# Copying each row of a column roll in three pieces instead of two

## Chip, cores, metric

One core of one Trainium2 chip. The metric is device time in microseconds, the median over runs. A ratio is the mean time of one kernel's fast runs over the mean of the fast runs of the kernel before from the same rounds on the same chip; it is therefore not quite the ratio of the medians quoted beside it. The bracket after a ratio is its 95% interval. A difference counts as faster or slower from 2% on.

## The reference

```python
x = np.random.randn(8192, 8192).astype(np.float32)   # 268 MB
shift = 100
np.roll(x, shift, axis=1)
```

Each row of 32768 B moves 400 B to the right, and its last 400 B come round to the front.

## The kernel before

There is no arithmetic and no on-chip buffer, only copies from HBM to HBM. Rows are taken in 16 chunks of 512, whose copies are issued by turns from two engines (SP and ACT, one DMA queue each). Every chunk has a long piece and a short piece.

```python
    s = shift % n_cols                      # 100
    engines = [nc.sync, nc.scalar]
    n_chunks = 16
    rows_per_chunk = n_rows // n_chunks     # 512
    for i in range(n_chunks):
        r0 = i * rows_per_chunk
        r1 = r0 + rows_per_chunk
        eng = engines[i % 2]
        eng.dma_start(out=out[r0:r1, s:], in_=x[r0:r1, : n_cols - s])
        eng.dma_start(out=out[r0:r1, :s], in_=x[r0:r1, n_cols - s:])
# ... launch code left out ...
```

In bytes, per row: a long piece of 32368 B is written from byte 400 of the output row to its end, and a short piece of 400 B is written to bytes 0 to 400. Byte 400 is 12.5 x 32. In what follows an edge of a write is called *even* if it falls on a multiple of 32 B of the output, and *ragged* if it does not. All ragged edges here are 16 B off. (Edges are counted from the start of a row. Rows are 32768 B long, and the tensor itself is taken to start on a multiple of 32 B; its address is not recorded.)

## Time and profile before

| | before |
|---|---|
| time before the prediction, median of 3 | 850.75 us (848.87 to 853.41) |
| span of the profiled run | 830.1 us |
| copied | 268.44 MB at 323 GB/s (647 GB/s read plus written) |
| long packets, 8192 of 32368 B | mean 1568 ns, 12% of them at 1199 ns |
| short packets, 8192 of 400 B | mean 35 ns, most at 24 ns |

The packet lines are worked out from the trace's packet records, which give each packet's queue, size, start and duration. Here one packet is one piece of one row. The profiled run is 20 us shorter than the timed runs; its chip is not recorded.

From the page of the kernel before: the span, the slices (busy tenths of the DMA engines and GB/s in 40 equal slices), the packets, the two queues (packets, MB, share of 16 engines' span) and the HBM traffic.

```profile
span 830.1 us, 77 instructions
...
DMA  9999999999999999999999999999999999999996
GB/s 306 324 326 315 328 322 323 331 329 328 334 323 334 338 311 340 324 334 334 306 339 324 332 329 314 328 331 335 329 305 335 332 328 326 311 334 328 329 326 208
DMA packets 16896, 268.44 MB, mean 323 GB/s; under 512 B 8704, under 2 KB 8704, under 8 KB 8704
...
q1 hardware_dynamic: 8448, 134.22, 49.8%
q10 hardware_dynamic: 8448, 134.22, 49.1%
HBM read 268.44 MB, written 268.44 MB: 647 GB/s over the span
```

The engines are hardly ever idle: 49.8% and 49.1% of their span add to 98.9%. A long packet takes 1199 ns at its quickest and 1568 ns in the mean. The GB/s row has shallow dips about every fifth slice, where chunks end (311, 306, 314, 305, 311; the first two chunk ends do not show at this width).

The chain of waits shows nothing here (0% in every entry): the only computing engine with any work is POOL, with 0.2 us. The timeline shows why issuing is not the limit. Its columns are start, duration, engine and line:

```profile
2.02 0.62 SPq L33 DMA_DIRECT2D out_dram<-in_x_dram  x1
2.28 0.85 ACTq L33 DMA_DIRECT2D out_dram<-in_x_dram  x1
2.69 94.08 SPq L34 DMA_DIRECT2D out_dram<-in_x_dram  x1
```

The third line is the fourth issue on SP. It lasts 94 us. What it waits for is not shown, but the DMA engines are working all that time: from 2.69 to 96.77 us the windows view gives a DMA share of 1.00 and 325 GB/s.

The first dip in stretches of 8 us, from the windows view of the kernel before (stretch, its length, POOL busy, clock, mean DMA share of the 16 engines, GB/s):

```profile
core 0: us, POOL busy (x), PEclk, DMA share, GB/s
88.00:96.00 8.00, 0.00 (x0) 1.00 0.93 332
96.00:104.00 8.00, 0.00 (x0) 1.00 0.99 308
104.00:112.00 8.00, 0.00 (x0) 1.00 1.06 294
112.00:120.00 8.00, 0.00 (x0) 1.00 0.98 344
120.00:128.00 8.00, 0.00 (x0) 1.00 1.06 348
...
102.00:110.00 8.00, 0.00 (x0) 1.00 1.01 237
```

The dip at 96 to 112 us is where the first two chunks end and their 1024 short packets run. Afterwards the rate is above the mean of 323 GB/s for a while (344 and 348), so little is lost. The view counts a packet, its bytes and its whole duration, in the stretch in which it starts; that is one way in which a share can pass 1 (the records also overlap). So where a stretch is cut matters: the last line, asked for separately, lies 2 us off the grid and shows 237 GB/s at the same dip.

### The profile page before, as it was taken

Reading aid. Unit: us, or ns where it says so; the run is one execution under the profiler, and the core shown is the slowest. Engines: PE = TensorE matmul, PEld = TensorE weight load, DVE = VectorE, ACT = ScalarE, POOL = GpSimd, SP = SyncE. Lnnn points to the kernel's source line nnn. Section 1 sums busy time; section 2 is a strip of 40 time slices with the busy share of each in tenths; the row PEclk is TensorE's granted clock in tenths of the full one; section 3 lists DMA queues with packets and bytes.
Section 4 is the critical chain, followed back from the end, with each engine's and each line's share of the span. In section 5 each row is a group of like instructions: output and inputs, shape, how many; then the busy total and the mean of one; then the engine's idle time right before and its main releaser. Section 6 shows DMA issues by size and latency. Waiting matters only on the chain. (4 is left out here: it accounts for less than half of the span.)

```text
span 830.1 us, 77 instructions
## 1 busy us (share of the span) xinstructions
POOL 0.2 (0%) x4
## 2 busy tenths in 40 slices
POOL 0000000000000000000000000000000000000000
DMA  9999999999999999999999999999999999999996
GB/s 306 324 326 315 328 322 323 331 329 328 334 323 334 338 311 340 324 334 334 306 339 324 332 329 314 328 331 335 329 305 335 332 328 326 311 334 328 329 326 208
DMA packets 16896, 268.44 MB, mean 323 GB/s; under 512 B 8704, under 2 KB 8704, under 8 KB 8704
## 3 DMA queue, kind: packets, MB, share of 16 engines
q1 hardware_dynamic: 8448, 134.22, 49.8%
q10 hardware_dynamic: 8448, 134.22, 49.1%
HBM read 268.44 MB, written 268.44 MB: 647 GB/s over the span
## 5 line engine op out<-in xcount | busy, mean ns | idle before, releaser
L51 POOL MEMSET const-bfloat16-1.0<- 128x1 bf16 x1 | 0.1, 102 | 0.0
L51 POOL MEMSET const-uint8-127<- 128x1 uint8 x1 | 0.1, 102 | 0.0
L51 POOL MEMSET const-float32-0.0<- 128x1 f32 x1 | 0.1, 99 | 0.2 <-issue 0.2
L51 POOL MEMSET const-float32-1.0<- 128x1 f32 x1 | 0.1, 99 | 0.0
## 6 DMA issues: line engine op xcount, KB each, us to landing
out_dram<-in_x_dram SPq DMA_DIRECT2D x8, 16184.0 KB, 206.1
out_dram<-in_x_dram ACTq DMA_DIRECT2D x8, 16184.0 KB, 206.3
out_dram<-in_x_dram ACTq DMA_DIRECT2D x8, 200.0 KB, 205.8
out_dram<-in_x_dram SPq DMA_DIRECT2D x8, 200.0 KB, 205.6
```

The costliest lines, as they stand in the source:

```text
L51: nc = _bacc.Bacc("TRN2", target_bir_lowering=False, num_devices=1)
```

## The change

The intent is a long piece that begins on a 512 B boundary of the output row. The 28 columns (112 B) from byte 400 to byte 512 become a third piece. The long piece is then 32256 B, and its source starts 112 B into the input row.

```diff
     s = shift % n_cols
+    a = -(-s // 128) * 128
+    pieces = [(a, a - s, n_cols - a), (0, n_cols - s, s), (s, 0, a - s)]
     engines = [nc.sync, nc.scalar]
     n_chunks = 16
-    rows_per_chunk = n_rows // n_chunks
+    rows = n_rows // n_chunks
     for i in range(n_chunks):
-        r0 = i * rows_per_chunk
-        r1 = r0 + rows_per_chunk
-        eng = engines[i % 2]
-        eng.dma_start(out=out[r0:r1, s:], in_=x[r0:r1, : n_cols - s])
-        eng.dma_start(out=out[r0:r1, :s], in_=x[r0:r1, n_cols - s:])
+        r = slice(i * rows, (i + 1) * rows)
+        for d, c, n in pieces:
+            if n > 0:
+                engines[i % 2].dma_start(out=out[r, d:d + n], in_=x[r, c:c + n])
```

(Blank lines and one comment that also changed are left out.)

## The prediction

> **What bounds the kernel now.** Data movement alone: the page's busy table shows 0.2 us of compute, and the queue lines put 49.8% and 49.1% of the 16 engines' span on the two queues, so the engines are never without work. The page gives 323 GB/s copied, 647 GB/s read plus written. The trace's packet records (one per row piece) say what the work is:
>
> - 8192 packets of 32368 B: 1199 ns at the shortest (12% of them), 1568 ns in the mean. Summed over 16 engines, 803 us.
> - 8192 packets of 400 B: 24 ns in most, 35 ns in the mean: 18 us.
>
> At their shortest these packets would need 626 us, an estimate from those durations[...].
>
> **What the change does.** The long piece of each row becomes 32256 B and starts on a 512 B boundary of the output; its source now starts 112 B into the row. The 400 B piece stays. A third piece of 112 B per row is added: 8192 more packets, 16 more DMA issues.
>
> - Hoped for: no ragged start of the long write. [...]32368 B at 1199 ns and 400 B at 24 ns differ by 27.2 B/ns[...]. The ragged boundary at byte 400 is still written from both sides. I expect almost no gain.
> - Long packets shorter by 112 B: 4 ns x 8192 / 16 = -2 us.
> - Added 112 B packets: estimate 13 ns at the shortest, from the 27.2 B/ns, and 25 ns with the stalls that the 400 B packets show: 8192 x 13..25 ns / 16 = +7 to +13 us. [...]around 100 us, in the short pieces, the rate falls from about 325 to 230 to 250 GB/s for 8 us.
>
> **On the critical path:** the engines are 98.9% busy, so the net +5 to +11 us lands on it, except where long packets[...] speed up in turn. Issue does not count: each sequencer waits 77 to 96 us per chunk.
>
> **Prediction:** 856 us (before: 850.75), 80% range 822 to 880. Faster by over 2%: 0.15; within 2%: 0.62; slower by over 2%: 0.23.
>
> **What would show the steps.** Right: packet records with 8192 of 112 B at 13 to 30 ns; long packets still near 1560 ns mean, shortest 1194 ns; longer GB/s dips at chunk boundaries. Wrong: the mean long packet well under 1540 ns, or GB/s outside the dips above 335: alignment matters all along the row.
>
> **What would make it wrong.** [...]small writes may cost far more than their engine time, or fewer chunks in flight (three pieces share the same number of completion semaphores) may leave engines idle at chunk boundaries: 2 to 4% slower.

The sum: -2 us for the shorter long packets and +7 to +13 us for the added ones make +5 to +11 us, and 856 us is the lower end, 850.75 + 5.

## More of the kernel before

The runs fell on several chips. The kernel before took 833 us on chip 15, 840 us on chips 9 and 0, and 852 us in the rounds of the result, whose chip is not recorded. Only ratios are compared across chips.

## The result and the profile after

| | before | after |
|---|---|---|
| median of 4 | 851.7 us (848.87 to 853.41) | 875.93 us (872.49 to 879.06) |
| ratio | | 1.0289 [1.0246, 1.0331], slower |

The same lines of the page, for the changed kernel:

```profile
span 876.7 us, 93 instructions
...
DMA  9999999999999999999999999999999999999995
GB/s 303 328 315 324 283 299 318 333 324 259 303 325 322 322 258 313 325 328 330 250 323 324 321 325 249 336 318 325 327 238 344 316 325 324 238 338 311 328 319 156
DMA packets 25344, 268.44 MB, mean 306 GB/s; under 512 B 17152, under 2 KB 17152, under 8 KB 17152
...
q1 hardware_dynamic: 12672, 134.22, 50.9%
q10 hardware_dynamic: 12672, 134.22, 48.5%
HBM read 268.44 MB, written 268.44 MB: 612 GB/s over the span
```

Between the dips the rate is about what it was, 299 to 344 GB/s in the slices. The dips are still every fifth slice, but now at 283, 259, 258, 250, 249, 238 and 238. The first of them in the windows view of the changed kernel:

```profile
core 0: us, POOL busy (x), PEclk, DMA share, GB/s
88.00:96.00 8.00, 0.00 (x0) 1.00 0.94 302
96.00:104.00 8.00, 0.00 (x0) 1.00 1.01 326
104.00:112.00 8.00, 0.00 (x0) 1.00 1.20 143
112.00:120.00 8.00, 0.00 (x0) 1.00 0.95 302
120.00:128.00 8.00, 0.00 (x0) 1.00 1.00 339
```

For 8 us the core moves 143 GB/s (237 in the lowest such stretch shown before), with a DMA share of 1.20. The engines are not idle; their packets take longer: in the packet records of the whole run 133 long packets took more than 3 us, against 2 before.

To compare runs, the time lost at the chunk boundaries is worked out from the packet records. It is the length of each stretch that holds short packets (with 8 us on either side) less the bytes moved in it over 325 GB/s. The sum is over the first seven boundaries; the eighth is the end of the run.

| | before | after |
|---|---|---|
| lost at seven boundaries | 4 us | 39 us |
| long packets: mean, total over 16 engines | 1568 ns, 803 us | 1625 ns, 832 us |
| 400 B packets: mean, total over 16 | 35 ns, 18 us | 44 ns, 23 us |
| 112 B packets: mean, total over 16 | none | 31 ns, 16 us |

So most of the added time went to the boundaries: 35 of the 46.6 us between the two profiled spans. Of the packet time that was added, 29 us lie in long packets and 16 us in the new packets themselves. The first profile flatters the kernel before, though. Profiled again (below), it lost 10 us at the seven boundaries and the changed kernel 34, and the rate outside the boundaries was 329 to 330 GB/s in both.

### The profile page after: what moved, and what is told of

Same layout as the page of the kernel before. It is cut to its first block, busy times and chain, and to the rows that moved or that the text cites. A ratio compares the mean times of both kernels' runs of the same rounds, so it can differ in the third digit from the quotient of the medians.

```text
span 876.7 us, 93 instructions
## 1 busy us (share of the span) xinstructions
POOL 0.2 (0%) x4
## 2 busy tenths in 40 slices
DMA packets 25344, 268.44 MB, mean 306 GB/s; under 512 B 17152, under 2 KB 17152, under 8 KB 17152
## 3 DMA queue, kind: packets, MB, share of 16 engines
HBM read 268.44 MB, written 268.44 MB: 612 GB/s over the span
```

## The experiments

The rival theories were these. (1) The added packets cost, and alignment of the long piece is worth nothing. (2) The moved misalignment costs, since the long read now starts ragged. (3) Alignment gains, but less than the packets cost. (4) With three issues per chunk and the same completion semaphores, fewer chunks are in flight. (Both traces show eight such semaphores, and four issues on each engine before the first long wait: on SP the fourth ends at 96.8 us before and at 97.6 us after.) If (1) held, the question was which property of the packets costs: number, size, edges or bunching. All edits below are to the list of pieces, (first output column, first input column, columns), in a loop like that of the changed kernel, unless said otherwise. The diffs are shortened and written against the changed kernel. The first four expectations name absolute times for a kernel before of 851 us; on the faster chip their results are read as ratios.

### The kernel before, profiled again: before_again

No edit.

> The kernel before, unchanged, for a second profile: the first profile's span (830 us) is about 20 us under the spans of its timed runs, so it may flatter the comparison. All theories: the time again near 851 us. The loss of moved bytes at each chunk boundary should again be under 2 us of time in the trace, against about 5 us in the changed kernel; if it is 4 us or more here, the boundaries are not what tells the two apart.

Measured: 836.38 us in one run, state unknown, on a chip where the kernel before had a median of 833.19 us. The boundaries lost 10 us in all, 0.9 to 2.2 us each. That is more than in the first profile (4 us) and far less than in the changed kernel (39 us), so the boundaries do tell the two apart. The time was not near 851 us as expected, on this other chip. The first profile's short span therefore says little; its chip is not known.

### The 112 B cut off at the other end: cut_at_end

```diff
-    pieces = [(128, 28, 8064), (0, 8092, 100), (100, 0, 28)]
+    pieces = [(100, 0, 8064), (0, 8092, 100), (8164, 8064, 28)]
```

> Same three sizes per row (32256, 400, 112 B) in the same order, but the 112 B are cut off at the row's end, so that the long piece still starts ragged at byte 400 of the output row and aligned in the input. Theory 1 (the added packets cost, alignment is worth nothing): as slow as the changed kernel, 870 to 880 us. Theory 2 (the moved misalignment costs: the long read now starts ragged): as fast as before, 848 to 858 us. Theory 3 (alignment gains, and the added packets cost even more): slower than the changed kernel, over 885 us.

Measured: 850.34 us against 833.19, ratio 1.020 [1.0152, 1.0247]. The absolute 870 to 880 us was written for a slower chip; as a ratio the result is close to the changed kernel's (1.0225 when that was run again, below). Here the long read is aligned again, and the kernel is still slow, so theory (2) falls. The boundaries lost 27 us. On this one chip the span grew by 14.3 us over before_again and the loss at the boundaries by 16 us, so the boundaries hold all of the difference.

### Without the third piece: no_third

```diff
-    pieces = [(128, 28, 8064), (0, 8092, 100), (100, 0, 28)]
+    pieces = [(128, 28, 8064), (0, 8092, 100)]
```

> The changed kernel without its 112 B piece; 28 columns of the output stay unwritten, so the result is wrong on purpose. Theory 1: as the kernel before within 1%, 843 to 857 us, and dips at the chunk boundaries as shallow as before's. Theory 2: still slower than before, 865 us or more. Theory 3: faster than before by over 2%, under 833 us.

The result is wrong (28 columns unwritten). Measured: 825.75 us against 833.19, ratio 0.9933 [0.9877, 0.999]. It moves 0.34% fewer bytes (28 of 8192 columns), which alone would give 0.9966 if time went with bytes (an estimate). The rest, 0.3%, is inside the interval. The long piece aligned to 512 B, with its read made ragged, thus gains nothing net that this run resolves, and by the interval's lower end at most about 0.9%. (Taken as an absolute time, 825.75 us would have met theory 3's "under 833 us"; but on this chip the kernel before itself takes 833 us.) Theory (3) falls, and the cost lies in the third piece. The boundaries lost 8 us, as in the kernel before.

### A third piece of 512 B with even edges: third_512

```diff
-    pieces = [(128, 28, 8064), (0, 8092, 100), (100, 0, 28)]
+    pieces = [(100, 0, 7964), (0, 8092, 100), (8064, 7964, 128)]
```

> Three pieces per row, but the third is 512 B, starting on a 512 B boundary of the output (bytes 32256 to 32768 of the row), and the long piece starts at byte 400 as in the kernel before. Theory 1a (what costs is one more packet in the burst, whatever its size): about as slow as the changed kernel, 868 to 885 us. Theory 1b[...]: back near before, 850 to 860 us. Theory 4 (fewer chunks in flight, since three issues per chunk share the completion semaphores): as slow as the changed kernel, like 1a, so this run does not tell 1a from 4.

Theory 1b, as far as it is tested here, says that something about the 112 B packets other than their number costs, such as their size or the place of their edges.

Measured: 836.46 us against 833.19, ratio 1.0034 [0.998, 1.0087]. As many packets, issues and semaphores as the changed kernel, and nearly no cost; the boundaries lost 9 us. Theories 1a (any packet more) and 4 (fewer chunks in flight) fall together. The 512 B packets took 40 ns in the mean, 21 us over 16 engines, more engine time than the 112 B packets of the changed kernel (16 us). Engine time of added packets is evidently not what the kernel pays.

### The changed kernel again: after_again

No edit; on one chip with the three runs that follow.

> The changed kernel unchanged, on the chip of the runs below and beside the kernel before. All theories: 1.02 to 1.033 of before. If it is within 1% of the ratio of the kernel whose third piece was cut at the row's end (1.02), the place of the 112 B piece does not matter[...].

Measured: 858.85 us against 839.53, ratio 1.0225 [1.0137, 1.0313]; 34 us lost at the seven boundaries. The interval holds both 1.020 and 1.0289, so nothing extra is shown for the 112 B piece lying next to the 400 B piece.

### Short but even: third_128_even

```diff
-    pieces = [(128, 28, 8064), (0, 8092, 100), (100, 0, 28)]
+    pieces = [(100, 0, 8060), (0, 8092, 100), (8160, 8060, 32)]
```

> As the kernel with the third piece cut at the row's end, but the third piece is 128 B and starts and ends on multiples of 64 B of the output; the long piece ends there.[...] Theory S (size: a write under 512 B is what costs): 1.012 to 1.028 of before. Theory P[...]: 0.997 to 1.006.

As tested, P says that a third piece costs if an edge of its write lies off such multiples, whatever its size.

Measured: 842.0 us against 839.53, ratio 1.0012 [0.9936, 1.0088]. The boundaries lost 7 us. This 128 B write costs nothing that the run resolves for being short. Theory S falls as the whole cause, and P stands. The 128 B packets' source starts 16 B off a multiple of 32 B, so this ragged read costs nothing either.

### Longer than 512 B but ragged: third_624_ragged

```diff
-    pieces = [(128, 28, 8064), (0, 8092, 100), (100, 0, 28)]
+    pieces = [(100, 0, 7936), (0, 8092, 100), (8036, 7936, 156)]
```

> As the run before, but the third piece is 624 B and starts 16 B off a multiple of 64 B of the output; the long piece ends there. Over 512 B[...]. Theory S: 0.997 to 1.007 of before, as the 512 B piece. Theory P: 1.012 to 1.028. If both this and the 128 B piece cost, the two causes add up; if neither does, only small and ragged together cost.

Measured: 847.44 us against 839.53, ratio 1.0084 [1.0016, 1.0151]; 19 us lost at the boundaries. The piece starts 16 B off a multiple of 64 B, and of 32 B too. The result falls between the two expectations, and by the 2% rule it is "same", though its interval is clear of 1. A ragged edge costs also at 624 B, but by the means less than half of what it costs at 112 B on the same chip (1.0225). Of all third pieces tried here, only those with a ragged edge have a cost clear of noise, and at 624 B it is smaller than at 112 B. Why is not explained by any run here.

### Long pieces on one queue, short ones on the other: after_split

```diff
     for i in range(n_chunks):
         r = slice(i * rows, (i + 1) * rows)
-        for d, c, n in pieces:
-            engines[i % 2].dma_start(out=out[r, d:d + n], in_=x[r, c:c + n])
+        for k, (d, c, n) in enumerate(pieces):
+            eng = nc.sync if k == 0 else nc.scalar
+            eng.dma_start(out=out[r, d:d + n], in_=x[r, c:c + n])
```

> The changed kernel's own pieces, every one of them, but all long pieces issued from SP and all short ones from ACT, so that short packets run beside long ones instead of filling both queues at a chunk boundary. Theory B (a burst of short packets on both queues at once is what costs): dips gone, 0.985 to 1.008 of before. Theory C (each short packet costs the same wherever it stands): still 1.018 to 1.035.

Measured: 858.05 us against 839.53, ratio 1.0229 [1.0142, 1.0316], so no change from the changed kernel. The windows view of this run:

```profile
0.00:48.00 48.00, 0.20 (x4) 1.00 0.97 312
48.00:64.00 16.00, 0.00 (x0) 1.00 1.15 177
64.00:84.00 20.00, 0.00 (x0) 1.00 1.34 88
84.00:100.00 16.00, 0.00 (x0) 1.00 1.14 224
100.00:140.00 40.00, 0.00 (x0) 1.00 1.00 322
140.00:156.00 16.00, 0.00 (x0) 1.00 1.04 180
156.00:200.00 44.00, 0.00 (x0) 1.00 1.00 329
200.00:400.00 200.00, 0.00 (x0) 1.00 1.00 331
400.00:800.00 400.00, 0.00 (x0) 1.00 1.00 332
```

The edit did not spread the short packets as I had meant it to; it bunched them differently. All 16384 of them ran in the first 152 us, and from 200 us on the rate is 331 to 332 GB/s. At 332 GB/s, 48 to 100 us lost 27 us and 140 to 156 us lost 7 us. Together that is about the 34 us that the changed kernel loses over seven of its eight boundaries. The cost moved with the packets, as theory C has it. Theory B is not settled, because most short packets stayed bunched. They were spread in one stretch only: from 100 to 140 us 400 packets of 112 B ran among 398 long ones, at 322 GB/s, where 40 us stretches after 160 us reach 327 to 339. That hints that spread packets are not free, but one stretch is little.

This run also shows the cost by itself. From 64 to 84 us the packet records start 3499 packets of 112 B, 3438 of 400 B and no long one. At their commonest durations (13 and 24 ns) these short packets would take (3499 x 13 + 3438 x 24) / 16 = 8.0 us of the 16 engines. They took 20 us. As many short packets passed faster elsewhere: in heads_by_sbuf (last experiment), where they are written to SBUF, 4096 of 112 B and 3123 of 400 B ran from 100 to 120 us together with 127 long ones, at 290 GB/s.

### 128 B with both edges ragged: third_128_ragged

```diff
-    pieces = [(128, 28, 8064), (0, 8092, 100), (100, 0, 28)]
+    pieces = [(132, 32, 8060), (0, 8092, 100), (100, 0, 32)]
```

> The changed kernel with its third piece made 128 B instead of 112: bytes 400 to 528 of the output row, so that it starts and ends 16 B off a multiple of 64 B, and the long piece starts at 528. Length as in the 128 B piece that cost nothing, place ragged. Theory place (what counts is where the short write starts and ends in the output): 1.015 to 1.035 of before. Theory length (what counts is a length that is no multiple of 64 B, as 112 and 624 are not): 0.997 to 1.006.

Measured: 866.63 us against 839.87, ratio 1.035 [1.0291, 1.041]. The place of the edges decides here, not the length: 128 B cost 3.5% here and 0.1% when even, and the boundaries lost 37 us here and 7 when even. The first boundary, windows view of the 128 B piece with even edges:

```profile
96.00:104.00 8.00, 0.00 (x0) 1.00 0.97 307
104.00:112.00 8.00, 0.00 (x0) 1.00 1.12 268
112.00:120.00 8.00, 0.00 (x0) 1.00 1.02 355
```

and of the 128 B piece with ragged edges:

```profile
96.00:104.00 8.00, 0.00 (x0) 1.00 1.00 303
104.00:112.00 8.00, 0.00 (x0) 1.00 1.29 139
112.00:120.00 8.00, 0.00 (x0) 1.00 0.95 330
```

268 GB/s against 139, with the same packet size and count. The long packets took 1560 ns in the mean in the first and 1604 ns in the second. The ragged piece has two ragged edges; that it costs more than the 112 B piece with one (1.035 against 1.020 to 1.029) fits a cost per edge, but its interval overlaps both of the changed kernel's, so a cost per edge is not shown.

### 96 B on a multiple of 32 B: third_96_half

```diff
-    pieces = [(128, 28, 8064), (0, 8092, 100), (100, 0, 28)]
+    pieces = [(100, 0, 8068), (0, 8092, 100), (8168, 8068, 24)]
```

> The third piece is the last 96 B of the output row: it starts on a multiple of 32 B that is no multiple of 64 B, and the long piece ends there. [...]

The forecast ranges were 1.012 to 1.03 of before if the edges have to lie on multiples of 64 B, and 0.997 to 1.006 if multiples of 32 B are enough.

Measured: 839.14 us against 839.87, ratio 0.9991 [0.9944, 1.0037]. The piece starts at byte 32672, which is 1021 x 32 and no multiple of 64. So here a multiple of 32 B sufficed.

### The 400 B piece cut to 384 B: short_384

In the kernel before (the run wrote the same copies as a list of pieces):

```diff
-        eng.dma_start(out=out[r0:r1, :s], in_=x[r0:r1, n_cols - s:])
+        eng.dma_start(out=out[r0:r1, :96], in_=x[r0:r1, n_cols - s:n_cols - 4])
```

> The kernel before with its short piece cut from 400 to 384 B, so that it ends on a multiple of 64 B; 4 columns of the output stay unwritten, so the result is wrong on purpose. The bytes shrink by 0.05%. If a ragged short write costs as much here as the 112 B piece did in the changed kernel: 0.975 to 0.985 of before. If the end of a 400 B write being ragged costs little: 0.993 to 1.0.

The result is wrong (4 columns unwritten). Measured: median 839.22 us against 839.87, ratio 0.9937 [0.9875, 0.9999]. Two of its six runs (827 and 831 us) were faster than the rest, and the ratio leaves out the two longest (840 and 841 us), which count as slow for lying over 1.5% above the fastest. With all six the means differ by 0.4%. By time alone the effect is not settled. The profile, which is of one of the two fast runs, shows the dips gone:

```profile
GB/s 301 326 325 326 322 325 337 320 336 319 342 331 325 336 312 343 328 328 328 321 335 332 328 336 325 334 317 325 332 327 339 326 336 328 323 335 331 326 325 213
```

No boundary loses time in it (the sum over seven is -2 us). So the kernel before's own shallow dips seem to come from the 400 B piece's ragged end, and by the interval they are worth 1.25% at most. The next run, which has no ragged 400 B write to HBM either, shows no gain.

### Heads of rows put together on the chip: heads_by_sbuf

```diff
     for i in range(n_chunks):
         r = slice(i * rows, (i + 1) * rows)
         eng = engines[i % 2]
+        g = i // 4                              # 4 groups of 2048 rows
+        if i % 4 == g % 2:
+            heads[g] = pool.tile([128, j, a], x.dtype, name="head")    # in SBUF; j = 16, a = 128
+            eng.dma_start(out=heads[g][:, :, :s], in_=of_group(x, g)[:, :, n_cols - s:])
+            eng.dma_start(out=heads[g][:, :, s:], in_=of_group(x, g)[:, :, :a - s])
         eng.dma_start(out=out[r, a:], in_=x[r, a - s:n_cols - s])
-        eng.dma_start(out=out[r, :s], in_=x[r, n_cols - s:])
-        eng.dma_start(out=out[r, s:a], in_=x[r, :a - s])
+        if i % 4 == 2 + g % 2:
+            eng.dma_start(out=of_group(out, g)[:, :, :a], in_=heads[g])
```

(`of_group(t, g)` views the 2048 rows of group g as 128 partitions of 16 rows.)

> The first 512 B of each output row are put together in SBUF by two loads (400 B and 112 B, as ragged in SBUF as in the changed kernel) and stored whole, aligned to 512 B; the long piece starts at byte 512 as in the changed kernel. Four packets per row instead of three. If the cost of ragged short writes sits where the output in HBM is written: 0.985 to 1.006 of before, so at least 1.6% better than the changed kernel, and if the 400 B piece pays too, faster than before. If it sits in the DMA engines' handling of ragged packets, or in the number of packets: 1.02 to 1.045.

Measured: 840.16 us against 839.87, ratio 1.0009 [0.9969, 1.0049]. The same 400 B and 112 B pieces with the same ragged meeting point, written to SBUF, cost nothing that the run resolves, although a fourth packet per row was added and 4.2 MB more moved. The 112 B packets took 13 ns in the mean here, which is their commonest duration everywhere, against 27 ns when written to HBM (after_again). So the cost (1.0225 in after_again, 1.0009 here) sits where ragged pieces are written to the output in HBM. It is no better than the kernel before, so the "faster than before" that was expected if the 400 B piece pays too did not come, and the complication does not pay: a ragged 400 B end is cheap enough to leave (at most 1.25%, short_384).

## Why the prediction was right or wrong

The range of 822 to 880 us held, by 4 us and because it was wide. The forecast's weight did not: 0.62 was on within 2%, and the measured +2.9% had been given 0.23. The forecast was +5 us, and the result was +24 us. What happened stands in the prediction among the ways in which it could be wrong, and not in its main line.

- **"I expect almost no gain" from the aligned long piece: right.** Without the third piece the aligned kernel stands at 0.9933, of which 0.34% are missing bytes. The argument for it was shown by no trace. The rate of 27.2 B/ns says nothing of alignment, since a penalty in proportion to length would lie in the rate itself. The changed kernel's trace shows that the quickest long packets kept their rate: 1193 ns for 32256 B with an aligned write and a ragged read, 27.0 B/ns, as 1199 ns for 32368 B the other way round before. The moved misalignment of the read did not matter either (1.020 in cut_at_end, where the read is aligned again, against 1.0225 in after_again).
- **"+7 to +13 us" for the added packets: this is the term that was mis-sized.** It took the packets' own duration as their price. Their own duration was 14 to 16 us over 16 engines. The price was 19 us (after_again, 858.85 less 839.53) to 24 us (the first rounds), and it was not that duration: 128 B even packets with 9.8 us of engine time and 512 B ones with 20.7 us cost 0.1% and 0.3%. In these runs the price goes with ragged edges of short writes (2.0 to 2.9% at 112 B, 3.5% at 128 B). The number of ragged edges is not it: two edges per row are ragged in the kernel before (both sides of byte 400) and two in the changed kernel, where one of them has passed from a 32 KB write to a 112 B write. Against the even 128 B piece on the same chip, after_again has 24 us more in long packets, 4 us more in the 400 B ones and 4 us more in the third piece. So most of that difference is paid by the packets beside it.
- **"The engines are 98.9% busy, so the net lands on it": wrong as reasoning.** Against the prediction's own 626 us at the shortest durations the packets took 821 us (803 + 18), so nearly 200 us of this busy time is packets taking longer than their quickest. I read that as waiting; what they wait for is not shown. Harmless packets displaced such waiting here. On one chip the long packets fell from 808 us over 16 engines (before_again) to 789 us with the 512 B even piece, about 10 us of it because they are 512 B shorter, while the new packets added 21 us. Harmful packets displaced none: with the ragged 112 B at the row's end (cut_at_end, same chip) the long packets stayed at 809 us, and the new packets' 13 us and 4 us more in the 400 B packets came on top.
- **"Longer GB/s dips at chunk boundaries": right**, and they hold most of the loss: 39 us after against 4 us before (34 against 10 when both were profiled again), with 326 to 330 GB/s outside the boundaries in all four profiles.
- **"Long packets still near 1560 ns": wrong**, 1625 ns, mostly through those of over 3 us (133 against 2; without them the mean is 1584 ns).
- **"Small writes may cost far more than their engine time": this is what happened**, for small ragged writes to HBM: 14 to 16 us of their own, 19 to 24 us in the kernel's time. **"Fewer chunks in flight": not the cause** (1.0034 in third_512, with as many issues).
- The page's HBM line gives exactly the copies' own bytes for both kernels (268.44 MB read and written). It shows no other traffic; whether it would count any is not known.

What is shown, for this kernel and for edges 16 B off, is that short writes to HBM with an edge off a 32 B multiple slow what moves beside them (1.020 to 1.0289 at 112 B, 24 us more in long packets in after_again than with the even 128 B piece), and that even ones of 96, 128 and 512 B cost nothing that the runs resolve (0.9991, 1.0012, 1.0034). Why a ragged edge costs is not shown. Nor is it tested whether one such edge costs alone: at every ragged edge of a third piece another write covers the rest of the same 32 B, so two writes that meet there could be what costs. Only for the 400 B piece is there a run without such a neighbour (no_third), and there the boundaries lost 8 us, as in the kernel before. Open is also why an edge of a 112 B write costs over twice that of a 624 B write (1.0225 against 1.0084).

## What to carry to other kernels

Before cutting a small piece off to align a large one, look at the edges that the small piece gets in HBM: here 8192 writes of 112 B with one edge 16 B off a 32 B multiple cost 2.0 to 2.9%, and the alignment bought for the 32 KB piece returned nothing measurable (0.9933 in no_third, of which 0.34% are missing bytes). In this copy, whose long packets took 1568 ns in the mean against 1199 ns at their quickest, a packet's own duration was no measure of its price (21 us of 512 B packets cost 0.3%, 16 us of 112 B ones 2.9%); look for what the long packets beside it do, in short windows around the place where it runs. If a ragged seam cannot be avoided, what cost less here was to let it lie between larger writes (0.8% at 624 B against 2.3% at 112 B, on one chip) or to join the pieces in SBUF (0.1%).
